# Low halves of eleven weight tiles by a negated copy and an accumulating DMA, and weights asked for two tiles ahead

## The chip, the cores and the metric

One core of a Trainium2 chip runs the whole layer. The metric is the device time of one execution in microseconds (us). The engines in the profile's names: PE (matrix products), DVE (vector operations), ACT (activations and copies), POOL (general purpose; here little more than an issuer of DMAs) and SP (issues most DMAs).

## What is computed

```python
h = rmsnorm(x, g_pre_mix) * (1 + sc1) + sh1            # x: 512 x 1024
proj = h @ w_in                                         # q, k, v of mixers a and b, indexer, two gates
isc = sum_h relu(q_i . k_i) * w_i ; causal ; top_k(isc, 128)
oa = softmax over the selected keys (qa . ka) @ va      # 8 heads of 64, sparse attention "a"
att = exp(log_sigmoid(z) + sum of log_sigmoid(-z) of the later keys)   # z = qb . kb, strictly causal
ob = att @ vb                                           # 8 heads, stick-breaking attention "b"
merged = sigmoid(gate_a) * (oa @ w_up_a) + sigmoid(gate_b) * (ob @ w_up_b)
x = x + ga1 * rmsnorm(merged @ w_out, g_post_mix)
u = relu((rmsnorm(x, g_pre_ffn) * (1 + sc2) + sh2) @ w_ff1)
x = x + ga2 * rmsnorm((u * u) @ w_ff2, g_post_ffn)
```

The six vectors sh1 to ga2 come from silu(c) @ w_ada + b_ada. The top 128 scores of each query row are found as 16 rounds of the eight largest.

## The kernel before

**Products in three parts.** A float32 operand is held as a high half (rounded to the format that PE multiplies) and a low half (what is left). Each product is three matmuls: high by high, high by low, low by high (`mm3`). A weight tile of 128x1024 is loaded by `stage` into one of three buffers `st` (line 109, SP's queue), and `split` makes the halves: ACT copies `st` into `whi` (L113), DVE subtracts, `wlo = st - whi` (L114). There are four buffers each of `whi` and `wlo` (`WBUF`). `wload` does this for one tile; `wnext` hands out the tiles of the list `srcs` in order and loads `AHEAD` = 1 tile further than the one asked for.

**The list of tiles.** First 6 tiles of the v weights (two times three, `V_CUTS`), then by `ORDER = "bbbgbggaggaggg"`: two tiles of w_b for each b (q and k of a pair of b heads), one of w_gate for each g, four of w_a for each a. After those, in the merge, w_gate and w_up for each of 8 column blocks m, and four tiles of w_out.

**The mixer stage** (about 60 to 320 us). Several generators take turns: the main stream of products, the indexer, the units of attention b and of attention a. From 104 us on DVE has two kinds of work. One is the indexer's top 128: per round and for each of three blocks of rows (256, 384 and 512 keys) a MAX8 (L411) and a MATCH_REPLACE8 (L412), and at the end `mask` (L416), which attention a needs. The other is attention b: for each unit (two heads, four blocks b of 128, 256, 384 and 512 keys) ACT writes the two sigmoids `a` (L484) and `be` (L485), DVE scans `a` (L486) and multiplies `be` by it (L488), PE transposes `be` (`tr`, L430), ACT evacuates it to `pT` (L185), and PE multiplies by v. The program code gives the order in which all this is issued, but the layer that records the program sorts each engine's instructions by estimates of its own, so that a change of one instruction can move others.

**The merge stage** (about 320 to 401 us). For each m: PE makes the gate product (24 matmuls into a bank `mm`), then `pb` (12 matmuls with `obh`, `obl`) and `pa` (12 with `oah`, `oal`) from one tile of w_up. Both go into banks of the tag `s`, of which there are three: in this order of use, pb of block m+1 takes the bank of pa of block m-1, and pa of m+1 that of pb of m. DVE reads pb in L676 and pa in L679. Between these DVE has the adaLN columns: up to four tiles of w_ada per m (`LATE`), each loaded through the same three `st` buffers and reduced by one DVE dot product (L213). After the last m come eight transposes (`tr<-identr,ga`), then the product with w_out into four banks; the fourth of these, `s_863`, is the bank that pb of m = 7 had.

The last stages (norm, w_ff1, w_ff2) also use `wload`, and their accumulating DMAs (`wn`, L890; `ub`) are issued by POOL.

Of the kernel before, what the change touches and what calls it, by code (L numbers as in the profile page):

```python
# [7 lines left out]
F32 = mybir.dt.float32  # L8
F32R = mybir.dt.float32r
BF16 = mybir.dt.bfloat16  # L10
AF = mybir.ActivationFunctionType
ALU = mybir.AluOpType
# [3 lines left out]
D = 1024  # L16
# [11 lines left out]
V_CUTS = ((0, 3), (3, 6), (6, 8))  # L28
# [21 lines left out]
EVAC_B = 100  # L50
NORM = 4
ORDER = "bbbgbggaggaggg"
AHEAD = 1
ROWS = 6
IDX_GAP = 1
# [10 lines left out]
def layer_kernel(tc, x, ada, vecs, c_row, rope, w_first, w_v, w_b, w_a, w_gate, w_up, w_out, w_ff1, w_ff2, w_right, out):  # L66
    nc = tc.nc
    es = ExitStack()
    with es:
# [5 lines left out]
        def uid(name):  # L75
            cnt[0] += 1
            return f"{name}_{cnt[0]}"
# [29 lines left out]
        def stage(src, w=D):  # L107
            st = per.tile([P, D], F32, name=uid("st"), tag="st", bufs=3)
            nc.sync.dma_start(st[:, :w], src)
            return st  # L110

        def split(dst_hi, dst_lo, src):
            nc.scalar.activation(dst_hi, src, AF.Copy)  # L113
            nc.vector.tensor_tensor(dst_lo, src, dst_hi.bitcast(F32), op=ALU.subtract)  # L114
# [1 line left out]
        wmore = []  # L116
        turn, wturn = [0], [0]

        def wload(src, w=D):
            st = stage(src, w)  # L120
            wturn[0] = (wturn[0] + bool(wmore)) % (WBUF + 1)
            if wmore and wturn[0] == 0:
                pair = wmore[0].tile([P, 2, D], F32R, name=uid("wx"), tag="ah")
                hi, lo = pair[:, 0], pair[:, 1]
            else:
                hi, lo = [per.tile([P, D], F32R, name=uid(n), tag=n, bufs=WBUF) for n in ("whi", "wlo")]
            split(hi[:, :w], lo[:, :w], st[:, :w])
            return hi, lo

        def scaled_gain(dst, j, g0):  # L130
# [134 lines left out]
        for k in range(KT):  # L265
            if k + 1 < KT:
                prepare(k + 1)
            hi, lo = wfirst[k]
# [223 lines left out]
        srcs = [(w_v[g, i, :, :(k1 - k0) * VREST], (k1 - k0) * VREST) for g in range(2) for i, (k0, k1) in enumerate(V_CUTS)]  # L492
        feeds = {"b": iter(w_b[i] for i in range(8)), "g": iter(w_gate[i] for i in range(8)), "a": iter(w_a[i] for i in range(8))}
        for kind in ORDER:
            srcs += [(next(feeds[kind]), D) for _ in range({"b": 2, "g": 1, "a": 4}[kind])]
# [3 lines left out]
        ready = []  # L499

        def wnext(i=[0]):
            while len(ready) < min(len(srcs), i[0] + 1 + AHEAD):
                ready.append(wload(*srcs[len(ready)]))
            i[0] += 1
            return ready[i[0] - 1]

# [10 lines left out]
        def pair_b(hp):  # L517
            qq = q_pair()
            kk = k_pair()
            def parts(ps, scale):  # L520
                hi, lo = [tp.tile([P, 512], F32R, name=uid(n), tag=n, bufs=2) for n in ("bhi", "blo")]
                nc.scalar.activation(hi, ps, AF.Copy, scale=scale)
                nc.vector.scalar_tensor_tensor(lo, ps, scale, hi.bitcast(F32), op0=ALU.mult, op1=ALU.subtract)
                return [(hi[e * HD:(e + 1) * HD], lo[e * HD:(e + 1) * HD]) for e in range(2)]

            ps = yield from cols_T(wnext())
            for e, (hi, lo) in enumerate(parts(ps, QK_SCALE)):
                r, o = slice(e * HD, (e + 1) * HD), slice((1 - e) * HD, (2 - e) * HD)
                nc.sync.dma_start(qq[r, e].bitcast(F32), hi.bitcast(F32))
                nc.sync.dma_start(qq[o, e].bitcast(F32), lo.bitcast(F32))  # L530
            yield
            ps = yield from cols_T(wnext())
            for e, (hi, lo) in enumerate(parts(ps, 1.0)):
                r, o = slice(e * HD, (e + 1) * HD), slice((1 - e) * HD, (2 - e) * HD)
                nc.sync.dma_start(kk[r, 2 * e].bitcast(F32), hi.bitcast(F32))
                nc.sync.dma_start(kk[o, 2 * e].bitcast(F32), lo.bitcast(F32))
                nc.sync.dma_start(kk[o, 2 * e + 1].bitcast(F32), hi.bitcast(F32))
                nc.sync.dma_start(kk[r, 2 * e + 1].bitcast(F32), lo.bitcast(F32))
            yield

            def ready():
                yield 2
                tens[f"b{hp}"] = [(qq[:, e], kk[:, 2 * e:2 * e + 2]) for e in range(2)]

            spawn(ready())

        def project(dst, scale):
            ws = [wnext(), wnext()]
            for t in range(NT):
                ts = slice(t * P, (t + 1) * P)  # L550
                ps = bank("mm")
                for k in range(KT):
                    hi, lo = ws[k // 4]
                    cs = slice((k % 4) * 256, (k % 4 + 1) * 256)
                    mm3(ps[:, :256], hTh[k][:, ts], hTl[k][:, ts], hi[:, cs], lo[:, cs], k == 0, k == KT - 1)
                    if k == 3:
                        yield
                nc.scalar.activation(dst[:, t], ps[:, :256], AF.Copy, scale=scale)
                if t == NT - 1:
                    do_rope(dst.rearrange("p t (h d) -> p t h d", h=4), 4)  # L560
                yield
# [35 lines left out]
        def main_stream():  # L597
# [4 lines left out]
            nb = ng = na = 0  # L602
            for kind in ORDER:
                if kind == "b":
# [61 lines left out]
        for m in range(KT):  # L666
# [3 lines left out]
            hi, lo = wnext()  # L670
# [50 lines left out]
        for k in range(KT):  # L721
            if k < WOB:
                wo.append(wnext())
            else:
                st = stage(w_out[k])
                hi = wp.tile([P, D], F32R, name=f"woh{k}")
                lo = wp.tile([P, D], F32R, name=f"wol{k}")
# [97 lines left out]
        def token_sums(p):  # L825
            nc.vector.tensor_tensor(blk(p, S3), blk(p, A11), blk(p, S1), op=ALU.subtract)
            nc.vector.tensor_tensor(blk(p, S1), blk(p, S1), blk(p, A22), op=ALU.subtract)
            nc.vector.tensor_tensor(blk(p, S2), blk(p, S1), blk(p, A11), op=ALU.subtract)

        ws = [wload(w_ff1[m]) for m in range(EARLY)]  # L830
        for h in range(2):
            for m in range(EARLY):
# [3 lines left out]
        for m in range(EARLY, MF):  # L836
            ff1(m, wload(w_ff1[m]), 0, NT)
            if m == MF - 1 - WBUF:
                wmore.clear()
            if m % 2:  # L840
                token_sums(m // 2)
                i = (m - 11) // 2
                if 0 <= i < KT:
                    ada_cols(40 + i)
                    gated_gain(KT + i, 40 + i, 72 + i)
                    if i == KT - 1:
                        rows_of(ga2b, ga[:, KT:], evac)
# [138 lines left out]
        for p in range(NP - LAST):  # L986
# [12 lines left out]
            if p in (5, 6):  # L999
                i = p - 5  # L1000
# [135 lines left out]
```

## Time and profile before

| | before |
|---|---|
| median of 3 runs (lowest to highest) | 788.04 us (787.72 to 788.55) |
| the profiled execution: its time, its span | 787.75 us, 785.9 us |
| granted PE clock, mean | 0.998 |
| PE busy, share of the span | 762.7 us, 97% |
| DVE busy | 582.5 us, 74% |
| ACT busy | 406.4 us, 52% |
| POOL busy | 28.6 us, 4% |

The span runs from the first to the last instruction of the profiled execution; its time lies 1.85 us above. Busy matmuls overlap in the profile (each lasts longer than the distance to the next), so the time that PE loses is read from the distances between starts, and from what it waited for.

### The profile page before, as it was taken

To read this page: it belongs to the slowest core of one execution; us is meant where nothing else is said; L and a number is where in the kernel's file an instruction comes from. 1 tells how busy PE (TensorE), PEld (TensorE's weight loads), DVE (VectorE), ACT (ScalarE), POOL (GpSimd) and SP (SyncE) were. 2 spreads that over 40 slices of the span, in tenths; PEclk is the share of its full clock that TensorE was granted. 3 is DMA by queue.
4 is the path that set the end of the run, shared out by engine and by line. 5 is a ranking of instruction groups with operands and counts; after the bars stand their busy time and mean duration, and the time that the engine had idled before them with its cause. 6 is when DMAs were issued, how large, how long until landed. Compare 5 with 4: busy or idle time off the path is not lost.

```text
span 785.9 us, 10955 instructions
## 1 busy us (share of the span) xinstructions
PE 762.7 (97%) x4014; PEld 636.8 (81%) x4014; DVE 582.5 (74%) x1096; ACT 406.4 (52%) x736; POOL 28.6 (4%) x44
## 2 busy tenths in 40 slices
PE   5999999998999999999999999999999999999996
PEld 5889988777889877786778898888888878888885
DVE  6966799999747678678875875554544588888966
ACT  6545546545647578623145863223232368768852
POOL 0000000000000000000000000000000011161000
PEclk9999999999999999999999999999999999999999
DMA  9943266450131210377784254434422189899502
GB/s 349 402 124 90 73 162 174 134 146 30 59 104 54 81 55 28 105 248 251 253 285 170 75 176 152 155 130 144 160 82 81 54 217 218 198 208 262 183 0 108
DMA packets 36437, 117.48 MB, mean 149 GB/s; under 512 B 4640, under 2 KB 4640, under 8 KB 36384
## 3 DMA queue, kind: packets, MB, share of 16 engines
q1 hardware_dynamic: 32064, 105.74, 40.2%
q0 software_dynamic: 4176, 11.01, 8.1%
q8 instruction: 32, 0.52, 0.3%
q14 instruction: 21, 0.17, 0.1%
q10 hardware_dynamic: 144, 0.03, 0.0%
HBM read 108.38 MB, written 2.10 MB: 141 GB/s over the span
## 4 chain that ended last, share of the span: by engine, by line
PE 73%; DVE 16%; DMA 6%; ACT 2%; issue 2%; SPq 0%; DVEq 0%; ACTq 0%
PE mm L140 24%; PE s L140 19%; PE o L140 7%; PE s L870 6%; PE mm L870 5%; PE tr L870 5%; DVE wlo L114 3%; DVE isc L412 3%; DVE sm L411 2%; DVE a L486 2%; DMA st<-in_ada_dram 2%; DMA st<-in_w_up_dram 2%; PE tr L430 2%; DVE st L213 1%; PE tr L140 1%
## 5 line engine op out<-in xcount | busy, mean ns | idle before, releaser
L113 ACT ACTIVATE whi<-st 128x1024 fp32r<-128x1024 f32 (+3 forms) x102 | 102.1, 1003 | 170.1 <-PE mm L140 44.9
L114 DVE TENSOR_TENSOR wlo<-st,whi 128x1024 fp32r<-128x1024 f32 (+3 forms) x102 | 117.3, 1153 | 60.8 <-ACT whi L113 60.7
L140 PE MATMUL mm<-hTh,whi 128*128 128x512 f32 x192 | 77.9, 406 | 0.0
L140 PE MATMUL mm<-hTh,wlo 128*128 128x512 f32 x192 | 75.4, 393 | 0.0
L140 PE MATMUL mm<-hTl,whi 128*128 128x512 f32 x192 | 75.1, 391 | 0.0
L140 PE MATMUL mm<-whi,hTh 128*128 128x256 f32 (+2 forms) x208 | 62.2, 305 | 0.0
L213 DVE CUSTOM_DVE_ANT_0 st<-st,cb,vec 128x1024 f32<-128x1024 f32 x32 | 41.0, 1283 | 26.4 <-DMA st<-in_ada_dram 26.2
L140 PE MATMUL mm<-whi,hTl 128*128 128x256 f32 (+2 forms) x208 | 60.2, 295 | 0.0
L140 PE MATMUL mm<-wlo,hTh 128*128 128x256 f32 (+2 forms) x208 | 60.1, 295 | 0.0
L140 PE MATMUL s<-h2h,whi 128*128 128x512 f32 (+1 forms) x120 | 43.4, 361 | 0.0
L140 PE MATMUL s<-h2l,whi 128*128 128x512 f32 (+1 forms) x120 | 43.3, 361 | 0.0
L140 PE MATMUL s<-h2h,wlo 128*128 128x512 f32 (+1 forms) x120 | 43.3, 361 | 0.0
L140 PEld LDWEIGHTS mm<-hTh,wlo 128*128 128x128 f32 x192 | 36.0, 188 | 7.7
L140 PEld LDWEIGHTS mm<-hTl,whi 128*128 128x128 f32 x192 | 36.2, 188 | 6.3
L140 PEld LDWEIGHTS mm<-hTh,whi 128*128 128x128 f32 x192 | 36.2, 189 | 6.2 <-issue 0.2
L140 PEld LDWEIGHTS mm<-wlo,hTh 128*128 128x128 f32 x208 | 39.5, 190 | 1.1
L140 PEld LDWEIGHTS mm<-whi,hTl 128*128 128x128 f32 x208 | 39.5, 190 | 0.6
L140 PEld LDWEIGHTS mm<-whi,hTh 128*128 128x128 f32 x208 | 39.0, 190 | 0.4
L870 PE MATMUL s<-whi,ah 128*128 128x512 f32 x100 | 36.1, 390 | 0.3 <-ACT whi L113 0.3
L890 POOL DMA_DIRECT2D wn<-in_w_right_dram x13 | 11.4, 874 | 577.6 <-DVE ub L909 528.0
L140 PE MATMUL s<-kT,qT 128*128 128x256 f32 (+2 forms) x128 | 30.6, 345 | 0.9 <-ACT be L485 0.9
L823 DVE TENSOR_TENSOR ub<-ub 128x512 f32<-128x512 f32 (+1 forms) x36 | 22.4, 626 | 10.8 <-ACT ub L822 10.8
(352 smaller groups left out, 1956.2 us busy)
## 6 DMA issues: line engine op xcount, KB each, us to landing
st<-in_w_ff_dram SPq DMA_DIRECT2D x50, 512.0 KB, 3.4
st<-in_ada_dram SPq DMA_DIRECT2D x32, 512.0 KB, 3.8
sa<-in_ada_dram SPq DMA_DIRECT2D x16, 512.0 KB, 8.6
st<-in_w_gate_dram SPq DMA_DIRECT2D x16, 512.0 KB, 3.7
ld<-in_w_ff_dram SPq DMA_DIRECT2D x14, 512.0 KB, 4.5
wn<-in_w_right_dram POOLq DMA_DIRECT2D x13, 512.0 KB, 5.9
st<-in_w_first_dram SPq DMA_DIRECT2D x8, 512.0 KB, 8.9
st<-in_w_b_dram SPq DMA_DIRECT2D x8, 512.0 KB, 3.4
```

The source lines that it names most:

```text
L113: nc.scalar.activation(dst_hi, src, AF.Copy)
L114: nc.vector.tensor_tensor(dst_lo, src, dst_hi.bitcast(F32), op=ALU.subtract)
L140: nc.tensor.matmul(o, lhsT, rhs, start=start, stop=stop)
L213: nc.vector.tensor_tensor_reduce(out=st, in0=st, in1=cb[0], scale=1.0, scalar=vec[:, j:j + 1], op0=ALU.mult, op1=ALU.add, accum_out=mod[:, ...
L411: nc.vector.max(out=m8, in_=cur)
L412: nc.vector.match_replace(out=cur, in_to_replace=m8, in_values=cur, imm_value=SENT)
L430: nc.tensor.transpose(tr[:, j * P:(j + 1) * P], ps[e][:, j * P:(j + 1) * P], ident)
L486: nc.vector.tensor_tensor_scan(a[:, n - 1::-1], a[:, n - 1::-1], zero.to_broadcast([P, n]), 1.0, op0=ALU.mult, op1=ALU.add)
L823: nc.vector.tensor_tensor(u, u, u, op=ALU.mult)
L870: nc.tensor.matmul(acc[i], s[:, ts], m[:, cs], start=f, stop=l, skip_group_check=onto)
L890: nc.gpsimd.dma_start(nw[p], w_right[p], accum_op=ALU.add)
```

## The change

Eleven tiles, number 6 to 16 of the list (the eight of w_b and the first three of w_gate), get their low half in another way: ACT writes `hi = copy(st)` and `lo = copy(-hi)`, and POOL issues a DMA that reads the tile from DRAM once more and adds it onto `lo`. DVE has no part in these tiles. From tile 6 on `wnext` asks two tiles ahead instead of one, in the mixer, in the merge and for w_out.

```diff
+N_V = 2 * len(V_CUTS)
+N_DMA = 11
 AHEAD = 1
...
-        def wload(src, w=D):
+        def wload(src, w=D, low_by_dma=False):
             st = stage(src, w)
...
-            split(hi[:, :w], lo[:, :w], st[:, :w])
+            if low_by_dma:
+                nc.scalar.activation(hi, st, AF.Copy)
+                nc.scalar.activation(lo, hi.bitcast(F32), AF.Copy, scale=-1.0)
+                nc.gpsimd.dma_start(lo, src, accum_op=ALU.add)
+            else:
+                split(hi[:, :w], lo[:, :w], st[:, :w])
             return hi, lo
...
         def wnext(i=[0]):
-            while len(ready) < min(len(srcs), i[0] + 1 + AHEAD):
-                ready.append(wload(*srcs[len(ready)]))
+            while len(ready) < min(len(srcs), i[0] + 1 + (AHEAD if i[0] < N_V else AHEAD + 1)):
+                n = len(ready)
+                ready.append(wload(*srcs[n], N_V <= n < N_V + N_DMA))
             i[0] += 1
             return ready[i[0] - 1]
```

The order of instructions moves at three places that matter here. Line numbers of the changed program are 2 to 8 higher than before (L418 there is L411 here, L419 is L412, L493 is L486, L495 is L488, L684 is L676, L687 is L679), and buffer numbers differ as well.

On DVE in the mixer, the last rows up to the product `be` of the third pair of heads, second head, block of 384 keys; before:

```order
L486 SCALAR_TENSOR_TENSOR a_367_1904<-a_367_1904,zero_87 128x384
L412 MATCH_REPLACE isc_78_585<-sm_425_2191,isc_78_585 128x512
L488 TENSOR_TENSOR be_368_1905<-be_368_1905,a_367_1904 128x383
L411 MAX sm_441_2260<-isc_78_585 128x8
L411 MAX sm_445_2292<-isc_78_585 128x8
L486 SCALAR_TENSOR_TENSOR a_370_1914<-a_370_1914,zero_87 128x384
L412 MATCH_REPLACE isc_78_585<-sm_441_2260,isc_78_585 128x256
L412 MATCH_REPLACE isc_78_585<-sm_445_2292,isc_78_585 128x384
L411 MAX sm_453_2328<-isc_78_585 128x8
L411 MAX sm_457_2365<-isc_78_585 128x8
L412 MATCH_REPLACE isc_78_585<-sm_453_2328,isc_78_585 128x512
L488 TENSOR_TENSOR be_371_1915<-be_371_1915,a_370_1914 128x383
```

and with the change:

```order
L495 TENSOR_TENSOR be_371_1922<-be_371_1922,a_370_1921 128x383
L418 MAX sm_480_2502<-isc_78_585 128x8
L493 SCALAR_TENSOR_TENSOR a_373_1931<-a_373_1931,zero_87 128x384
L419 MATCH_REPLACE isc_78_585<-sm_480_2502,isc_78_585 128x512
L418 MAX sm_491_2560<-isc_78_585 128x8
L418 MAX sm_492_2569<-isc_78_585 128x8
L419 MATCH_REPLACE isc_78_585<-sm_491_2560,isc_78_585 128x256
L419 MATCH_REPLACE isc_78_585<-sm_492_2569,isc_78_585 128x384
L418 MAX sm_496_2596<-isc_78_585 128x8
L495 TENSOR_TENSOR be_374_1932<-be_374_1932,a_373_1931 128x383
L419 MATCH_REPLACE isc_78_585<-sm_496_2596,isc_78_585 128x512
L423 TENSOR_SCALAR mask_606<-isc_78_585 128x256
```

The same `be` (`be_371` before, `be_374` now) stands behind 14, 13 and 13 MAX8 (256, 384, 512 keys) and 13, 13 and 13 MATCH_REPLACE8 before, and behind 16, 16 and 16 and 16, 16 and 15 now; of the splits since the first MAX8 there are 9 before and 3 now.

On SP in the merge, the loads through the three `st` buffers for one m; before:

```order
L109 DMA st_783_3898<-in_w_up_dram 128x1024
L109 DMA st_787_3930<-in_w_gate_dram 128x1024
L109 DMA st_792_3968<-in_ada_dram 128x1024
L109 DMA st_793_3972<-in_ada_dram 128x1024
L109 DMA st_794_3976<-in_ada_dram 128x1024
L109 DMA st_795_3980<-in_ada_dram 128x1024
```

and with the change:

```order
L111 DMA st_773_3829<-in_w_gate_dram 128x1024
L111 DMA st_777_3861<-in_w_up_dram 128x1024
L111 DMA st_782_3899<-in_ada_dram 128x1024
L111 DMA st_783_3903<-in_ada_dram 128x1024
L111 DMA st_784_3907<-in_ada_dram 128x1024
L111 DMA st_785_3911<-in_ada_dram 128x1024
```

In each round of six the w_up tile is now that of the next m, so that it comes a whole round earlier for PE; one w_up tile more stands ahead of the first w_ada tiles.

On DVE at the end of the merge, around the read of the last pb (L676, now L684); before:

```order
L114 TENSOR_TENSOR wlo_841_4270<-st_839_4267,whi_840_4269 128x1024
L213 ISA st_844_4305,mod_91<-st_844_4305,cb_746_3652,vec_65 128x1024
L213 ISA mod_91 128x1
L114 TENSOR_TENSOR wlo_849_4341<-st_847_4338,whi_848_4340 128x1024
L676 TENSOR_TENSOR mrg_748_3657<-s_843_4274,mrg_748_3657 128x512
```

and with the change:

```order
L116 TENSOR_TENSOR wlo_844_4287<-st_842_4284,whi_843_4286 128x1024
L220 ISA st_847_4322,mod_91<-st_847_4322,cb_749_3669,vec_65 128x1024
L220 ISA mod_91 128x1
L116 TENSOR_TENSOR wlo_852_4358<-st_850_4355,whi_851_4357 128x1024
L684 TENSOR_TENSOR mrg_751_3674<-s_846_4291,mrg_751_3674 128x512
```

The read of the last pb keeps its place behind the same number of loads; only the tiles are others (w_out 1 and 2 instead of 0 and 1).

## Rows read from the trace of the kernel before

**Rows 1.** What PE waited for: us in total, times, longest.

```profile
PE tr L430 <- ACT pT L185: 3.5, 3, 2.8
...
PE s L140 <- DVE wlo L114: 2.1, 4, 0.5
PE s L140 <- ACT whi L113: 1.3, 3, 0.7
```

**Rows 2.** Busy time per engine in two stretches: PE, PEld, DVE, ACT, POOL, clock, DMA.

```profile
104.00:200.00 96.00, 91.81 (x527) 73.43 (x527) 95.75 (x223) 49.68 (x117) 0.60 (x2) 1.00 0.45 124
335.00:401.00 66.00, 62.44 (x266) 48.96 (x265) 53.30 (x86) 16.78 (x23) 0.00 (x0) 1.00 0.78 254
```

**Rows 3.** Timeline of PE at the longest wait in the mixer: start, duration, [idle before].

```profile
184.26 0.88 PE L430 MATMUL tr<-identr,be 128*128 128x128 f32 x6 [2.76 <-ACT pT L185]
```

**Rows 4.** Timeline of ACT ahead of that wait.

```profile
180.93 0.60 ACT L485 ACTIVATE be<-s 128x512 f32<-128x512 f32 x1 [2.35 <-DVE be L488]
```

**Rows 5.** Chain of waits, 100 to 200 us: start, length, link.

```profile
104.20 0.79 DVE sm L411 x2
104.99 0.92 DVE isc L412 x2
105.91 0.92 DVE sm L411 x2
106.83 1.06 DVE isc L412 x2
...
111.45 1.05 DVE sm L411 x2
...
164.50 1.12 DVE wlo L114
...
193.91 1.19 DVE isc L412 x2
```

**Rows 6.** Timeline of DVE as the indexer's top 128 begins.

```profile
100.76 1.23 DVE L114 TENSOR_TENSOR wlo<-st,whi 128x1024 fp32r<-128x1024 f32 x1 [0.86 <-ACT whi L113]
...
104.13 0.87 DVE L411 MAX8 sm<-isc 128x8 f32<-128x256 f32 x2
```

**Rows 7.** Timeline of ACT: high half of tile 10, an evacuation, high half of tile 13.

```profile
99.67 1.06 ACT L113 ACTIVATE whi<-st 128x1024 fp32r<-128x1024 f32 x1 [0.55 <-PE mm L140]
100.63 0.58 ACT L522 ACTIVATE bhi<-mm 128x512 fp32r<-128x512 f32 x1
...
117.85 1.06 ACT L113 ACTIVATE whi<-st 128x1024 fp32r<-128x1024 f32 x1 [1.00 <-PE mm L140]
```

**Rows 8.** The accumulating DMAs of `wn`, 512 KB each: ns on POOL, and landing.

```profile
L890 POOL DMA_DIRECT2D wn<-in_w_right_dram x13: 862/862/1011, 632.6 to 692.7; - x13
...
DMA to landing us min/median/max: 5.4/5.9/7.9
```

**Rows 9.** Loads into `st` from 326 to 396 us: landing, min/median/max.

```profile
DMA to landing us min/median/max: 3.2/4.3/5.3
```

**Rows 10.** Timeline of PE in the merge and into the w_out product.

```profile
340.63 0.39 PE L140 MATMUL mm<-hTh,whi 128*128 128x512 f32 x1
...
346.07 0.39 PE L140 MATMUL s<-obh,whi 128*128 128x512 f32 x1
...
401.01 1.03 PE L154 MATMUL tr<-identr,ga 128*128 128x128 f32 x8
...
403.95 0.39 PE L140 MATMUL s<-whi,mgh 128*128 128x512 f32 x1
```

**Rows 11.** Timeline of DVE at the start and the end of the merge.

```profile
324.30 1.23 DVE L162 TENSOR_TENSOR cb<-cb,cs 128x1024 f32<-128x1024 f32 x1 [0.80 <-ACT cs L161]
...
402.95 0.68 DVE L676 TENSOR_TENSOR mrg<-s,mrg 128x512 f32<-128x512 f32 x1
```

**Rows 12.** Timelines of SP and PE: last copy of the first `kT`, and its first use.

```profile
112.46 0.59 SPq L538 DMA_DIRECT2D kT<-blo  x1
...
116.01 0.28 PE L140 MATMUL s<-kT,qT 128*128 128x256 f32 x1
```

## The prediction

> **What bounds the kernel now.** I read the first part of the page (PE is busy nearly all the span), then the list of PE's waits, then busy time by stretch, then the chain of waits and the timelines at the places that these name. The list shows where PE can still gain: it waited for ACT's evacuation of the transposed `be` of attention b (3.5 us, one wait of 2.8), and in the merge for the halves of a w_up tile (2.1 and 1.3 us) [rows 1]. The change touches both. The stretches show that the limits there differ [rows 2]. From 104 to 200 us DVE is busy 95.75 of 96 us, so PE's waits there come from DVE's queue: the longest ends at 184.26 [rows 3], and ahead of it ACT's next sigmoid had waited 2.35 us for DVE's `be` of 383 keys, which ended at 180.9 [rows 4]. From 335 to 401 DVE is busy 53 of 66 us, and the loads through three `st` buffers set the pace.
>
> The list understates the merge. 24 matmuls of a gate product take 346.07 - 340.63 = 5.44 us, 0.2267 each; from the first matmul of pb of m = 3 to the transposes are 216 matmuls, 48.96 us, but 54.94 pass [rows 10]. So 5.98 us are lost there, the slow restart after each wait included. That is the largest sum that the second half of the change could win.
>
> **The mixer, part by part.** Gone from DVE are eleven splits; six of them lay between the first MAX8 (104.13) and the `be` that ends at 180.9, nine before and three now (orders above). In the chain one split counts 1.12 us [rows 5], so 6.7 us leave this queue. But the order also shows what takes their place. Ahead of the same `be` there are now 2 more MAX8 of 256 keys, 3 more of 384, 3 more of 512, and 3, 3 and 2 more MATCH_REPLACE8. The chain has them in pairs [rows 5]: MAX8 0.79 (256 with 384), 0.92 (512 with 256), 1.05 (384 with 512); MATCH_REPLACE8 0.92, 1.06 and 1.19 in the same pairs. That is 0.79 + 0.92 + 2 x 1.05 = 3.81 and 2 x 0.92 + 1.06 + 1.19 = 4.09, together 7.9. So the queue ahead of this `be` grows by 7.9 - 6.7 = 1.2 us: the freed time goes to the top 128, whose mask comes earlier, and nothing waits for the mask there. Against this, the top 128 can begin earlier. The split at 100.76 goes [rows 6], and the instruction behind it needs only ACT's evacuation, which ends at 100.63 + 0.58 = 101.2 [rows 7] instead of 101.9: 0.6 us. Net the `be` ends 0.6 us later, and ACT's order between it and PE's transposes is the same, so the wait of 2.76 us ends 0.6 later. Waits before it are absorbed in it. Later ones shrink, since from the next pair of heads on the top 128 is finished and all 6.7 us are gained; of the two small waits in the 3.5 [rows 1], 0.7 together, I count 0.3 as gone. Mixer: +0.3 us. Bounds: -4 if the relief did reach PE, +3 if ACT's inserted copies leave DVE waiting three times for a copy of 1.06.
>
> **What is added.** Eleven negating copies on ACT, each like a `whi` (1.06 us [rows 7]); ACT is busy 50 of 96 us in the stretch [rows 2], and no copy stands between the late `be` and PE's wait. Cost nothing. The DMAs: the nearest rows are those of `wn`, the same 512 KB added onto a tile: 0.86 us on POOL, 5.9 to landing, 7.9 at most [rows 8]. Cover: the high half of tile 10 is written at 99.67, as soon as PE has released tile 6's buffers; the product of tile 10 follows that of tile 9, which ends just before tile 13's half is written at 117.85 [rows 7]. Of these 18.2 us the two copies take 2.1, the place of the second copy in ACT's order at most one product (6.1, a third of the 18.2), POOL 0.9, landing 5.9: 15.0. About 3 us are left at worst, 9 when the second copy follows at once. Cost nothing, on this cover. POOL's own other work there is three selections on the indexer's scores, between which one DMA stands; 0.9 us at most, and I take nothing, since the selection behind it serves only the third MAX8.
>
> **The merge.** The w_up halves now come a round of six loads earlier, so the five waits of [rows 1] on `wlo` and their companions on `whi` vanish, and PE could reach the transposes 5.98 us sooner. The ring itself doesn't run faster: six loads through three buffers are two landings (4.3 us median [rows 9]) with one split and one dot product behind them, and none of that waits for PE. And the product with w_out, after the transposes, needs a fourth bank, `s_863`, which pb of m = 7 had; its release is DVE's read L676, which stands in DVE's order behind the same ring loads as before. Before, that read ended at 402.95 + 0.68 = 403.63 [rows 11], and PE's first matmul into the bank came at 403.95 [rows 10], 0.3 later, without a wait. So PE, almost 6 us early, stops there until the read is done. The ring starts later now: one more w_up tile's split is ahead of DVE's multiplication at 324.30, 1.12 us, of which 0.80 fill idle time [rows 11]: +0.3. The read ends at 403.9, PE goes on at 404.0. Six us of waits vanish and one wait of about the same length takes their place: merge +0.1 us. Bounds: each load's landing can be a us off its median [rows 9], which passes to PE in full; -1.5 to +1.
>
> Behind this, w_out's own tiles come a slot earlier, and the later stages run as before.
>
> Sum: +0.3 + 0.1 = +0.4 on the profiled 787.75; the median of the three runs lies 0.29 above it, so 788.4 us. About 0.2% (1.6 us) is what a measurement can tell from no change; this is within it.
>
> **The rivals.**
>
> 1. The relief works. DVE has no slack in this stretch, and the order is by the recorder's estimates; if the chip's `be` came earlier nonetheless, because MAX8 rows are skipped over by waits of their own, the 3.5 us and most of a further us behind them go: 788.04 - 4.4 + 0.1 = about 783.7. Against it: an engine runs its order, and the counts are plain. The Trainium skill, "Perfetto Trace Analysis", Optimizing Scalar/DVE Operations, says that work may be moved to Scalar when DVE is saturated; by that alone the 6.7 us would be PE's as far as it waits. The trace agrees that DVE is saturated (95.75 of 96 us); what the freed time is spent on the rule doesn't say. 0.09.
>
> 2. The merge keeps part of its 6 us, because the ring, whose splits of w_up and gate stand in another order, ends 1.5 to 3 us sooner; then 785.4 to 786.9. For it: landings of 3.2 occur [rows 9]. Against: order and dependences of the ring are otherwise the same. 0.13.
>
> 3. Slower: the copies of `kT`. The last of the first set is issued at 112.46 and used at 116.01 [rows 12], 3.55 us later, and tile 11's accumulating DMA is under way just then. It decides if the copy then takes over 3.55 us; if it landed like `wn` after 5.9, PE would stop for 2.4 us and attention b, which feeds the saturated DVE, would begin that much later: 790.8. 0.13.
>
> 4. Slower: the accumulating DMAs land late. It decides above 5.9 + 3 = 9 us; each tile is triggered by the release of the tile four before, so that 2 us too many cost 2 us twice or three times over: 792 to 795. Against it: 7.9 is the maximum of 13 [rows 8]. The Trainium skill, "SBUF — State Buffer", on two separate sides ("DVE blocks DMA" trap), says that GpSimd can't write the descriptors of its DMAs while DVE holds the port that they share in certain modes. The rows of `wn` show 862 to 1011 ns on POOL, no sign of it; they come from a stretch where DVE was less busy than here. 0.07.
>
> **How the numbers follow.** The forecast has 0.58, with a range of its own of 787.2 to 789.9 (ring -1 to +1, mixer -0.5 to +1); most of it is within 1.6 us of 788.04, 0.05 of it above. Rivals 1 to 4 have 0.09, 0.13, 0.13, 0.07. Faster: 0.09 + 0.11 of rival 2 = 0.20. Slower: 0.13 + 0.07 + 0.05, less 0.02 of rival 3 that stays within = 0.23. Same: 0.57. The range reaches to rival 2's low end, 785.4, and to rival 3's 790.8; outside are rival 1, rival 4 and the edges of 2 and 3, a little under 0.2.
>
> **What would show it.** Right: the list of PE's waits loses `wlo` L114 and `whi` L113 of the merge and gains one of about 6 us (5 to 6.5) on DVE's read of pb (now L684) near 398 to 404; the transposes of the merge begin near 395.5; the mask is written 11 us earlier than 195; the wait of 2.8 on `pT` is still there, ending near 184.9. Wrong: a `be` of the third pair that ends before 180; a transpose wait under 2 us; no wait at the w_out bank; a `wlo` of tiles 6 to 16, or a `kT`, in PE's list.

## The result, and the profile after

The changed kernel takes 797.58 us (median of 4 runs, 797.25 to 799.08), beside 787.88 (787.65 to 788.55) for the kernel before on the same chip: ratio 1.0127, 95% interval 1.0115 to 1.0139. It is 9.7 us slower; I had forecast 788.4 and a range to 790.8. The profiled execution has a span of 795.4 us, 9.5 more than before.

What PE waited for, in the changed kernel; it answers to [rows 1]:

```profile
PE tr L437 <- ACT pT L192: 4.5, 2, 3.9
...
PE s L147 <- DMA kT<-bhi: 3.8, 1, 3.8
PE s L147 <- DVE mrg L684: 3.8, 1, 3.8
...
PE mm L147 <- ACT mrg L677: 0.7, 1, 0.7
...
PE s L147 <- DMA kT<-blo: 0.6, 1, 0.6
```

The merge's `wlo` and `whi` are gone, as the change means it. The copies of `kT`, on which PE never stopped before, are in the list, and the wait for `pT` has grown. The places, in PE's timeline of the changed kernel; the rows answer to [rows 3, 10, 12]:

```profile
113.25 0.39 PE L147 MATMUL mm<-hTh,wlo 128*128 128x512 f32 x1
117.41 0.55 PE L147 MATMUL s<-kT,qT 128*128 128x256 f32 x1 [3.77 <-DMA kT<-bhi]
118.52 0.55 PE L147 MATMUL s<-kT,qT 128*128 128x256 f32 x1 [0.56 <-DMA kT<-blo]
...
191.19 0.69 PE L437 MATMUL tr<-identr,be 128*128 128x128 f32 x2 [3.86 <-ACT pT L192]
...
353.95 0.39 PE L147 MATMUL s<-obh,whi 128*128 128x512 f32 x1
...
402.91 1.04 PE L161 MATMUL tr<-identr,ga 128*128 128x128 f32 x8
...
405.36 0.50 PE L147 MATMUL mm<-whi,mgh 128*128 128x512 f32 x1 [0.72 <-ACT mrg L677]
...
410.76 0.79 PE L147 MATMUL s<-whi,mgh 128*128 128x512 f32 x1 [3.75 <-DVE mrg L684]
```

In the kernel before, the last product ahead of the first `kT`, and that first use (PE's timeline):

```profile
114.15 0.39 PE L140 MATMUL mm<-hTh,wlo 128*128 128x512 f32 x1
114.38 0.40 PE L140 MATMUL s<-kT,qT 128*128 128x256 f32 x2
```

Ahead of the wait that ends at 191.19, `be` on DVE and two of ACT's sigmoids behind it, from the timelines of these two engines ([rows 4] has the first of these sigmoids before):

```profile
186.36 0.54 DVE L495 TENSOR_TENSOR be<-be,a 128x383 f32<-128x383 f32 x1
...
186.93 0.60 ACT L492 ACTIVATE be<-s 128x512 f32<-128x512 f32 x1 [2.73 <-DVE be L495]
...
189.78 0.60 ACT L492 ACTIVATE be<-s 128x512 f32<-128x512 f32 x1 [0.82 <-DVE be L495]
```

The second of them in the kernel before, where it had no wait:

```profile
182.85 0.60 ACT L485 ACTIVATE be<-s 128x512 f32<-128x512 f32 x1
```

Busy time by stretch in the changed kernel (columns as in [rows 2]); the first two rows answer to it:

```profile
104.00:200.00 96.00, 86.50 (x460) 68.74 (x459) 84.11 (x205) 50.63 (x113) 5.19 (x6) 0.95 0.65 164
335.00:401.00 66.00, 66.00 (x293) 54.66 (x292) 54.56 (x92) 17.63 (x24) 0.00 (x0) 1.00 0.76 250
100.00:115.00 15.00, 13.64 (x61) 10.93 (x59) 14.66 (x41) 8.67 (x12) 4.18 (x6) 1.00 1.05 281
...
116.00:118.00 2.00, 0.55 (x1) 0.29 (x1) 0.49 (x2) 0.00 (x0) 0.00 (x0) 0.50 1.08 212
118.00:120.00 2.00, 1.48 (x5) 1.23 (x6) 0.45 (x3) 0.45 (x2) 0.00 (x0) 0.50 1.01 255
...
191.00:193.00 2.00, 1.81 (x9) 1.81 (x10) 1.90 (x3) 1.42 (x5) 0.00 (x0) 0.50 0.40 127
...
410.00:412.00 2.00, 1.24 (x3) 1.05 (x4) 1.97 (x5) 1.06 (x1) 0.00 (x0) 0.50 0.82 279
```

And the stretch from 100 to 115 us in the kernel before, same view:

```profile
100.00:115.00 15.00, 15.00 (x70) 12.50 (x70) 14.24 (x35) 6.84 (x11) 1.55 (x3) 1.00 0.60 151
```

Two columns are new to the story. The DMA share of this stretch went from 0.60 to 1.05. The share adds up the times of the packets; since rows above 1 occur, 1 isn't its hard top, but by this measure the sixteen DMA engines are crowded. And the granted clock falls to 0.50 (1.2 of 2.4 GHz) behind each of the three long waits of PE.

To see where the time went I set the start of the same PE instruction in the two traces side by side (the difference is called the lag).

- **Before the first `kT`.** The lag is -0.9 from 20 us on (113.25 against 114.15 in the rows): the changed kernel's trace runs ahead there, long before its first accumulating DMA. The traces of the experiments stand at -0.7 to +1.0 at this place, so I take it for a difference between executions.
- **The copies of `kT`.** The two waits (4.33) and the matmuls at half clock behind them (2.7) bring the lag to 6.1.
- **The late transposes.** At those of 184.26 it is 191.19 - 184.26 = 6.93, 0.9 more than just ahead of them. The `be` of 383 keys isn't the cause: it ends at 186.90, 6.0 later than before, no more than PE was late itself. The 0.9 came behind it, where ACT's second sigmoid waited 0.82 for DVE's next `be`. Half clock adds 1.45, and 0.5 comes back near 208 us: 7.9 when the mixer is done.
- **The merge** gives 5.98 back (353.95 - 346.07 = 7.88, then 402.91 - 401.01 = 1.90).
- **In front of w_out** the two waits for evacuations bring it to 410.76 - 403.95 = 6.81, and half clock 2.7 more: 9.53, which stays to the end.

So 6.8 us are matmuls at half clock, in three places, against a net loss of 9.5.

### The profile page after: what moved, and what is told of

It reads as the page before. It is cut to its first block, busy times and chain, and to the rows that moved or that the text cites. A ratio compares the mean times of both kernels' runs of the same rounds, so it can differ in the third digit from the quotient of the medians.

```text
span 795.4 us, 10990 instructions
## 1 busy us (share of the span) xinstructions
PE 766.4 (96%) x4014; PEld 641.5 (81%) x4014; DVE 571.3 (72%) x1085; ACT 416.1 (52%) x747; POOL 38.2 (5%) x55
## 4 chain that ended last, share of the span: by engine, by line
PE 78%; DVE 10%; DMA 7%; ACT 3%; issue 2%; SPq 0%; DVEq 0%; ACTq 0%
PE mm L147 29%; PE s L147 19%; PE o L147 7%; PE s L878 6%; PE mm L878 5%; PE tr L878 5%; DMA st<-in_ada_dram 2%; PE tr L437 2%; DVE wlo L116 2%; DVE isc L419 1%; DVE sm L418 1%; DVE st L220 1%; PE tr L147 1%; PE tr L343 1%; DMA st<-in_w_up_dram 1%
## 5 line engine op out<-in xcount | busy, mean ns | idle before, releaser
L115 ACT ACTIVATE whi<-st 128x1024 fp32r<-128x1024 f32 (+3 forms) x91 | 90.4, 996 | 156.1 <-DMA st<-in_w_gate_dram 35.8
L116 DVE TENSOR_TENSOR wlo<-st,whi 128x1024 fp32r<-128x1024 f32 (+3 forms) x91 | 103.9, 1145 | 61.9 <-ACT whi L115 61.9
L493 DVE TENSOR_TENSOR_SCAN a<-a,zero 128x128 f32<-128x128 f32 (+3 forms) x32 | 25.6, 811 | 13.0 <-ACT a L491 13.0
```

What stands on the lines that cost most here:

```text
L493: nc.vector.tensor_tensor_scan(a[:, n - 1::-1], a[:, n - 1::-1], zero.to_broadcast([P, n]), 1.0, op0=ALU.mult, op1=ALU.add)
```

## The experiments

The kernel before was timed with each group: 787.98 us (e1, e2, e3, e5), 787.78 (e6, e8, e9, e10), 787.96 (e11, e12, e14, e16). Ratios are against it. The first group ran on another chip than the two others.

### The two halves apart

**e1** asks for weights early but leaves all splits on DVE; **e2** has the DMAs and asks one tile ahead everywhere.

```diff
 e1:
-N_DMA = 11
+N_DMA = 0
 e2:
-            while len(ready) < min(len(srcs), i[0] + 1 + (AHEAD if i[0] < N_V else AHEAD + 1)):
+            while len(ready) < min(len(srcs), i[0] + 1 + AHEAD):
```

> No low half by DMA (N_DMA = 0), two tiles ahead kept. Theory T (the accumulating DMAs' traffic delays the copies of kT): no wait on kT, the mixer as before, and at 335 us PE stands within 0.5 us of before; in the merge the five small waits on the w_up halves are gone, and one wait of 3.5 to 4 us for DVE's read of pb comes at the fourth w_out bank, with the granted clock at 0.5 for some 5 us after it; about +1.5, so 789 to 790. Rival O (the loads asked for earlier on SP's queue make kT late): the wait on kT stays, 794 to 796.

> Low halves of eleven tiles by DMA, one tile ahead as before. T: the wait on kT of about 4 us with the clock drop behind it, mixer +7 to +9 at 335 us; the merge as before with its small waits; 795 to 797. Rival O: no wait on kT, 788 to 789.

e1: 788.31 us, 1.0002 (0.9991 to 1.0012). e2: 795.22, 1.0094 (1.0074 to 1.0114). In e2 PE waits 2.9 us for `kT` and its lag is 7.6 at 208.9, 7.0 from 396. So 7.2 of the 9.7 us come with the DMAs alone and 0.3 with the earlier asking alone; about 2 appear only with both (e14). In e1 the merge gives 5.98 us, and the two waits ahead of w_out take 4.4 back; most of the rest goes to the clock (e10).

### What of the DMAs costs the time

**e3** leaves the second read out: the low half is the negated high half.

```diff
-                nc.gpsimd.dma_start(lo, src, accum_op=ALU.add)
```

> The changed kernel without the accumulating DMAs: the low half of the eleven tiles is left at the negated high half, all else (ACT's copies, DVE's order, two ahead) as changed. T: no wait on kT, its copies land in 2.2 to 2.5 us again; the wait on pT in the third pair of heads ends 0.6 to 0.9 later than before and may cost a clock drop; with the merge's +1.5 in all 789.5 to 791.5. Rival A (the reordering of DVE and ACT's extra copies cause most of the loss): 795 to 798.

789.34 us, 1.0022 (1.0007 to 1.0036). No wait for `kT`; DMA share 0.60 from 100 to 115, copies of `kT` landing in 2.2 to 3.8 us. ACT's eleven extra copies and DVE's new order cost about 1 us together (789.34 - 788.31, e1; the two spreads overlap). In e3's trace the mixer has none of it: the lag is 1.0 at 125 us and 1.0 at 335, and the wait at the w_out bank is 4.8 us, where e1 has 4.0. The read costs the rest, 8.2 us.

**e6** keeps the read, on the same queue and of the same size, but without adding (the low half then holds the weights).

```diff
-                nc.gpsimd.dma_start(lo, src, accum_op=ALU.add)
+                nc.gpsimd.dma_start(lo, src)
```

> The changed kernel with the second read of the eleven tiles left on the same queue and of the same size, but writing over the low half in place of adding to it (the low half then holds the weights themselves; only that is wrong in the output). Two theories of what made everything on the DMA rings land in 7 to 9 us. A, the accumulation: without it the copies of kT land in 2 to 3.5 us as in the kernel before, the kT wait of 3.8 us is gone, and the time is that of the kernel with the low half left negated and no second read, 789.3 (788 to 791). B, the bytes and the queue alone (5.8 MB more through GpSimd's queue): the copies of kT land in 7 to 9 us as in the changed kernel, and the time is 796 to 798.

796.21 us, 1.0107 (1.0090 to 1.0124): theory A, that the adding is the cause, fell. How long the copies of `kT` took to land (min, median, max, issues from 105 to 123 us), in the kernel before:

```profile
DMA to landing us min/median/max: 2.2/2.3/2.5
```

In the changed kernel:

```profile
DMA to landing us min/median/max: 7.3/8.8/9.3
```

In e6:

```profile
DMA to landing us min/median/max: 4.2/6.8/7.1
```

The adding makes the landing about 2 us longer, but a plain read is enough: PE waits 2.6 us for `kT` in e6. What a transfer takes of the engines stands in the page's list of queues (packets, MB, share of sixteen engines' span). The kernel before:

```profile
q1 hardware_dynamic: 32064, 105.74, 40.2%
q0 software_dynamic: 4176, 11.01, 8.1%
```

The changed kernel, whose eleven DMAs are the difference in q0:

```profile
q0 software_dynamic: 5760, 16.78, 11.9%
```

(0.119 x 795.4 - 0.081 x 785.9) / 11 = 2.8 us of all sixteen engines for one accumulating DMA; 1.9 for e6's plain one (10.7%); 1.6 for 512 KB on SP's queue (q1). Three of them are issued from 100 to 115 us: 3 x 2.8 / 15 = 0.56, on top of the 0.60 that was there. That is 1.16 by this sum; 1.05 was measured.

**e12** tests this by size: each DMA over half of the columns (the other half of the low part stays the negated high half). **e16** tests the place: only tiles 10 to 12, those three. **e8** does the opposite, tiles 6 to 9.

```diff
 e12:
-                nc.gpsimd.dma_start(lo, src, accum_op=ALU.add)
+                nc.gpsimd.dma_start(lo[:, :w // 2], src[:, :w // 2], accum_op=ALU.add)
 e16:
-                ready.append(wload(*srcs[n], N_V <= n < N_V + N_DMA))
+                ready.append(wload(*srcs[n], N_V + 4 <= n < N_V + 7))
 e8:
-N_DMA = 11
+N_DMA = 4
```

> The changed kernel, each of the eleven accumulating DMAs over half of the columns only (256 KB in place of 512; the other half of the low part stays the negated high half). Theory, the transfers' volume: with three accumulating DMAs of 512 KB in the stretch from 100 to 115 us the sixteen DMA engines have more to move than they can (share 1.05, against 0.60 before); with half of it the share falls to 0.8 to 0.9, the first copies of kT land in 3 to 5.5 us in place of 7 to 9, PE's wait for kT is 0 to 1.5 us, and the time is 789 to 792. Rival: any accumulating DMA under way delays everything, whatever its size: landings of 6 us and more, kT wait above 2.5 us, 794.5 to 797.

> The changed kernel with accumulating DMAs for the tiles 10, 11 and 12 only (three in place of eleven). Theory: the loss belongs to the place, the first copies of kT, and these three transfers are the ones under way there; so three of eleven bring nearly all of it: kT waits of 3 to 4.4 us, DMA share above 0.9 from 100 to 115, 793.5 to 797. Rival: each DMA costs its part: 788.3 + 3/11 of 9 = 790.7 or less.

> The changed kernel with four accumulating DMAs (w_b tiles 6 to 9) in place of eleven, all issued before the first kT copies. If the loss comes from accumulating DMAs that are under way just when the first kT copies are issued (my theory), there is no kT wait above 0.5 us and the time is that of the kernel with the earlier asking alone, 788.3, up to 1 us more for the other order of DVE: 787.5 to 790. If the loss goes with their number (a rate, each DMA costing its part), four elevenths of 7.2 to 9 us: 790.6 to 791.5.

e12: 789.72 us, 1.0026 (1.0007 to 1.0044). Its ten times go from 787.59 to 791.92, five of them above 790.9 at a mean clock of 0.991; the trace is of one at 788.09 (0.993). It has one wait for `kT`, of 0.4. Its stretch, DMA share 0.92, above the 0.8 to 0.9 that I expected (0.60 + 3 x 1.6 / 15 by its own q0 row would be 0.92):

```profile
100.00:115.00 15.00, 14.63 (x67) 11.89 (x66) 14.40 (x40) 9.08 (x14) 4.18 (x6) 1.00 0.92 230
```

and the landing of its `kT` copies:

```profile
DMA to landing us min/median/max: 2.2/3.5/5.2
```

e16: 795.52 us, 1.0102 (1.0085 to 1.0119). Three DMAs of eleven bring 7.6 us, most of the loss; its DMA share from 100 to 115 is 0.86, though, below the 0.9 that I expected. Its list of waits:

```profile
PE s L147 <- DVE mrg L684: 4.1, 1, 4.1
PE s L147 <- DMA kT<-blo: 4.1, 2, 2.2
...
PE tr L437 <- ACT pT L192: 2.4, 1, 2.4
```

e8: 789.11 us, 1.0015 (1.0001 to 1.0029), no wait for `kT`. Its own four reads slow other transfers too (the `qT` copies land in 5 to 6 us), but they are over when the copies of `kT` are issued:

```profile
DMA to landing us min/median/max: 2.2/2.3/3.4
```

So most of the loss belongs to three transfers at one place, not to a rate for each.

The share from 100 to 115 us doesn't put these runs in order: e8, without a wait, has more than e16. Over the microseconds in which the first copies of `kT` are issued and awaited, 106 to 118 (a window chosen afterwards), it does so much better:

| run | DMA share, 100 to 115 us | 106 to 118 us | PE's wait for `kT`, us |
|---|---|---|---|
| before | 0.60 | 0.65 | none |
| e1 | 0.59 | 0.64 | none |
| e3 | 0.60 | 0.65 | none |
| e8 | 0.94 | 0.81 | none |
| e12 | 0.92 | 0.87 | 0.4 |
| e6 | 0.91 | 0.97 | 2.6 |
| e16 | 0.86 | 1.00 | 4.1 |
| e2 | 1.05 | 1.07 | 2.9 |
| changed | 1.05 | 1.07 | 4.3 |
| e14 | 1.06 | 1.07 | 4.4 |

That the copies' packets stand behind those of the reads in the sixteen engines is the likely way; no view here shows it.

### The mixer: why DVE's relief gives nothing

**e11** is e3 with 13 of the 16 rounds of the top 128, so that DVE's order has no more rounds ahead of the late `be` than before, and six splits fewer.

```diff
-            for i in range(TOPK // 8):
+            for i in range(TOPK // 8 - 3):
```

> The kernel with eleven negated low halves and no second read, and with 13 of the 16 rounds of the top 128 (the top 104, so the mask is another one). Now as many rounds stand ahead of the be of 383 keys in DVE's order as in the kernel before (13), and six splits fewer. Theory (step of the prediction: the freed time goes to the top 128, and only therefore nothing comes of it at PE): this be ends 6 to 7 us earlier than in the kernel with 16 rounds, PE's wait of 2.8 to 3.0 us for pT near 184 falls under 0.5, and the time is 3 to 4.4 us below that kernel's 789.3: 785 to 786.3. Rival: PE's wait has another cause (ACT's own order, PE's banks), it stays above 2 us, 788.5 to 789.5.

785.59 us, 0.9975 (0.9963 to 0.9987), 3.75 below e3. The later `be` of the pair in e3's timeline of DVE:

```profile
181.85 0.54 DVE L494 TENSOR_TENSOR be<-be,a 128x383 f32<-128x383 f32 x1
```

and in e11's:

```profile
174.86 0.56 DVE L494 TENSOR_TENSOR be<-be,a 128x383 f32<-128x383 f32 x1 [0.35 <-ACT be L491]
```

7.0 us earlier, of which 1.3 is a difference of the two executions that stands from 20 us on. The wait near 184 (2.95 in e3) is gone, one of 1.3 for `pT`, earlier, is left in its list, and PE reaches the transposes of 184.26 at 181.27, 3.0 before the kernel before. So the relief is worth 3 to 4 us here, and the top 128 takes it.

### The merge: a bank, a split and the clock

**e10** is e1 with sixteen matmuls that nobody reads, in front of the matmul that waits for its bank. It asks whether the clock falls there because PE stands still.

```diff
+FILL_MM = 16
...
+                    if (k, t, n) == (0, 1, 1):
+                        fill = bank("o")
+                        for _ in range(FILL_MM):
+                            mm(fill, hTh[0][:, :P], hTh[1], True, True)
```

> Weights asked for two tiles ahead without any accumulating DMA, and sixteen matmuls of 128x512 added (3.6 us of work that nobody reads, into a bank of its own) just before the w_out matmul that waits 4.0 us for its bank. Theory: the granted clock fell to 0.5 behind that wait since PE stood still for 3.8 to 4 us, and this cost 2.6 us; with PE busy there the clock stays at 1.0 behind it and the time is 785.2 to 786.5 (2.6 below the same kernel without the added matmuls, 788.3). Rival: the clock falls there for another reason (then the row of the windows still shows 0.5 near 412, and the time is 788 to 789.5).

789.02 us, 1.0015 (1.0003 to 1.0027): not the time that I expected, but the clock did what the theory says. e1's stretches:

```profile
400.00:402.00 2.00, 0.00 (x0) 0.00 (x0) 1.26 (x2) 0.71 (x1) 0.00 (x0) 0.80 0.85 268
402.00:404.00 2.00, 1.38 (x3) 1.17 (x4) 1.97 (x4) 1.13 (x2) 0.00 (x0) 0.50 0.97 365
404.00:406.00 2.00, 2.00 (x6) 1.56 (x5) 1.90 (x3) 0.84 (x2) 0.00 (x0) 0.50 0.96 303
```

e10's, with PE busy:

```profile
400.00:402.00 2.00, 1.70 (x8) 1.12 (x7) 2.00 (x3) 1.06 (x1) 0.00 (x0) 1.00 0.58 193
402.00:404.00 2.00, 2.00 (x11) 1.60 (x10) 1.97 (x4) 0.63 (x1) 0.00 (x0) 1.00 0.71 246
404.00:406.00 2.00, 2.00 (x10) 1.68 (x9) 1.90 (x4) 1.35 (x2) 0.00 (x0) 1.00 0.47 135
```

This trace is of an execution at 787.22; the twelve times go from 786.74 to 791.24, most of them at a mean clock a little below its 0.999, so it doesn't show what the longer ones met. In it PE keeps 2.39 us of lead behind the bank (start 401.56, before 403.95); at 455 us it has 0.45 left. The next wait takes it, 1.7 us on DVE's `h2f` at the second norm. In the median the sixteen matmuls gain nothing.

**e5** takes the bank away instead: the fourth w_out bank comes from tag "o". **e9** does that too and gives out the third weight buffer of the feed-forward stage only behind the w_out stage.

```diff
 e5 and e9, on e1:
-        yt = [[bank(a), bank(b)] for a, b in (("mm", "mm"), ("s", "s"))]
+        yt = [[bank(a), bank(b)] for a, b in (("mm", "mm"), ("s", "o"))]
...
-        w_out_tile(2, ("s", "o"))
+        w_out_tile(2, ("s", "s"))
 e9 only:
-        wmore.append(x1p)
...
+        wmore.append(x1p)
```

> e1 with the fourth w_out bank taken from the tag o instead of s (and the next row block's second bank from s), so that it needs no read of pb. Theory M (the merge's gain was given back at this bank): the wait for DVE's read is gone, PE keeps most of the 6 us, less 1 to 2 us of waits for the third w_out tile, no clock drop: 783 to 785. Rival: the ring of loads sets the end of the w_out product anyway, and the wait moves to its tiles in full: 787 to 789.

> Weights asked for two tiles ahead without any accumulating DMA, the fourth w_out bank taken from another tag, and the third weight buffer of the feed-forward stage given out only behind the w_out stage, so that DVE's queue doesn't stand behind that load's split ahead of the first yg. If that split was what held DVE in the run before it (theory: PE keeps the merge's gain once nothing in DVE's order waits for a load there), PE keeps 3.5 to 5 us and the time is 783 to 785.5, and no wait on h2f of more than 1.5 us. Rival: the next thing in the order (first transposes of the second norm, which need all of w_out's tile on ACT and DVE) or a later feed-forward load takes it back: 787 to 789.

e5: 789.31 us, 1.0017 (1.0003 to 1.0030), not the 783 to 785 that I expected. The wait at the bank is gone, and a wait of 4.1 on `h2f` stands some 35 us later, ending at 438.2, with the clock at 0.50 behind it. The cause is in DVE's timeline:

```profile
423.07 1.23 DVE L116 TENSOR_TENSOR wx<-st,wx 128x1024 fp32r<-128x1024 f32 x1 [5.97 <-ACT wx L115]
424.21 0.68 DVE L709 TENSOR_TENSOR yg<-mm,ga1b 128x512 f32<-128x512 f32 x1
```

DVE stands 6 us in front of the split of a feed-forward weight that isn't loaded yet (ACT's copy of it waits 6.14 us for the load), and the evacuation of w_out's first tile (`yg`) is queued behind it: at 424.21, later than the 422.55 of the kernel before, though PE was 3.6 to 5 us early. In e9 the split stands further back, and the first `yg` is at 418.53:

```profile
418.53 0.69 DVE L709 TENSOR_TENSOR yg<-mm,ga1b 128x512 f32<-128x512 f32 x1 [2.17 <-ACT jk L708]
```

e9: 783.57 us, 0.9951 (0.9937 to 0.9966), 4.2 us faster than the kernel before; a wait of 1.0 on `mrg` and one of 0.7 on `xn` are all that the merge and the second norm still cost PE, and the clock stays at 1.00. It keeps the earlier asking and drops the accumulating DMAs.

**e14** puts e9's two edits on the changed kernel with all eleven DMAs.

> The changed kernel, all eleven accumulating DMAs, with the two changes of the merge that let PE keep its gain (fourth w_out bank of another tag, third weight buffer of the feed-forward stage given out behind the w_out stage). If the two halves of the change add up, it is the 783.6 of the kernel with these and without the DMAs, plus what the DMAs alone cost (795.2 - 788.0 = 7.2): 790 to 791.5. If the merge's gain hangs on the mixer's end (later loads, fewer under way), 787 to 789 or 792 to 794.

793.26 us, 1.0070 (1.0053 to 1.0086), above what I expected, though not for the rival's reason: the edits of the merge give 4.3 here (797.58 - 793.26) and 4.7 without DMAs (788.31 - 783.57), so they add up whenever the mixer ends. What doesn't is my price of the DMAs: 7.2 when tiles are asked for one ahead (e2), but 9.3 and 9.7 two ahead (797.58 - 788.31, 793.26 - 783.57). The traces put most of this at `kT`: the lag grows there by 5.5 us in e2, with the clock at 0.50 for 3.4, and by 7.0 in the changed kernel and 7.6 in e14, with 0.50 for 6.8. Why the clock stayed low longer isn't shown.

## Why the prediction failed, step by step

- **"What is added", failed.** "Cost nothing, on this cover." The cover that I worked out was that of the low half itself, and it held: the five accumulating DMAs issued from 96 to 128 us landed in 6.8 to 9.9 us, median 9.1, and no low half of tiles 6 to 16 is in PE's list. What I didn't count is what the transfers take from others. From 100 to 115 us they crowd the sixteen engines (1.05), the copies of `kT` land in 7.3 to 9.3 us in place of 2.2 to 2.5, and 3.55 us of cover [rows 12] is gone. PE lost 7.0 us there, 4.33 waiting and 2.7 at half clock. e3, e6, e12 and e16 show it: with no read, the read plain, half of it, three of them. A `kT` in PE's list was also the prediction's own sign of being wrong.
- **Rival 3 named the place but not the size.** I let a copy land like one `wn` DMA, 5.9 [rows 8], for 2.4 us of wait. PE waited 4.33, and at the first half of the set already (copies issued from 106.86 to 109.41), not only at the last copy; rival 3 had no clock in it either. The whole came to 7.2 (e2). The numbers for a better price were on the page before: q0 gives 0.081 x 785.9 us for 11.01 MB, 3.0 us of all engines for 512 KB, three times in a stretch whose share was 0.60.
- **Rival 4 didn't decide.** Landing beyond 9 us did occur, but no tile was late for its own product by it.
- **POOL's issue and the shared port, right.** These DMAs took 862 to 877 ns on POOL while DVE was busy 14.66 of 15 us. The Trainium skill's "DVE blocks DMA" trap ("SBUF — State Buffer", SBUF: two separate sides), which I weighed there, doesn't show; whether DVE's instructions here hold the shared port isn't in the trace.

From the tile's view of the changed kernel, for these two points:

```profile
L132 POOL DMA_DIRECT2D wlo<-in_w_b_dram x4: 862/869/877, 96.8 to 127.8; - x4
...
DMA to landing us min/median/max: 6.8/9.1/9.9
```

- **The mixer's own term: right in e3, near by luck in the changed kernel.** Forecast +0.6 at the late transposes and -0.3 behind. e3 has this order without the reads, and there these transposes come 0.5 later (a lag of 1.5, of which 1.0 was there from 20 us on), with 0.5 back behind them. In the changed kernel the +0.9 comes from ACT's second sigmoid, between the late `be` and PE's transposes, where the prediction had ACT's order unchanged. e11 shows the cause in DVE's order, and so that rival 1's relief is real but spent.
- **The merge, right in mechanism, two sizes off.** (The prediction reads five waits on `wlo` out of [rows 1]; the rows have four, and three on `whi`.) 216 matmuls from 353.95 to 402.91 are 48.96 us, just the working time that I had counted, so all of the 5.98 was won. The wait at the w_out bank came, but as 4.0 in e1, since DVE's read of pb started at 401.88, 1.07 earlier than before, where I had it 0.3 later:

```profile
400.74 1.23 DVE L116 TENSOR_TENSOR wlo<-st,whi 128x1024 fp32r<-128x1024 f32 x1 [1.88 <-ACT whi L115]
401.88 0.68 DVE L684 TENSOR_TENSOR mrg<-s,mrg 128x512 f32<-128x512 f32 x1
```

  Rival 2 had a ring that ends earlier for its gain. The clock took it away: in e1 PE is 1.33 us early at the bank and 1.36 late a few microseconds on. The term of +0.1 was nearly right for e1 (+0.3) by two errors that cancel.
- **The clock, missing.** The prediction prices each wait by its length. The one long wait that I had looked at, 2.76 [rows 3], leaves the clock at 1.00, and I took it as the pattern for all. In the changed kernel 6.8 us are lost to matmuls at half clock, against 9.5 in all. The Trainium skill, "TensorE: Matmul & The Clock Gate", "HAM oscillation — how this bites in real kernels", says that a PE which waits for DMA between bursts is throttled to half rate and starts the next burst cold. The rows of the three long waits agree, for waits on DMA, on ACT and on DVE alike; e10, with PE kept busy, is at 1.00. Some shorter waits here didn't lower it (last section).

## What to carry to other kernels

A transfer that nobody waits for isn't free: price it in engine time (its bytes by its queue's share in the page) and look at every small copy that will be under way beside it and has only a few us of cover. Add the price to the DMA share of just the microseconds in which such copies are under way: here 0.81 cost nothing, 0.87 a wait of 0.4 us, 0.97 and more 2.6 to 4.4. Three reads at such a place cost most of what eleven did. Where a wait is taken away, ask what stands next in the order of the engine that PE will then wait for (here a bank, then a split of a feed-forward weight), and follow it until nothing in that order waits for a load. And a wait that ended in a clock at 0.50 cost its length and 1.4 to 2.7 us more in the changed kernel.

## What I had not expected of the hardware

- Reads of 512 KB on GpSimd's queue, one every 5 to 6 us, delayed SP's copies of 128 KB by 4 to 5 us even when they added nothing (e6). The Trainium skill, "DMA: Bandwidth & Descriptors", "Issuing engines are not separate DMA queues", says that transfers of all issuers run on the same sixteen engines and interleave; the landings agree, and put a size on it: 2.3, 6.8 and 8.8 us (medians) with none, plain and accumulating reads beside them. Whether the same bytes on SP's own queue would do as much was not tried; with a single load of 512 KB on it directly ahead of the copies (e3) they landed in 2.2 to 3.8 us.
- One accumulating DMA of 512 KB took 2.8 us of all sixteen engines, a plain one on the same queue 1.9, 512 KB on SP's queue 1.6 (by the page's shares).
- Waits of nearly one length leave the clock in different states. The one for `pT` was 2.76 (before), 2.77 (e1) and 2.95 (e3) with the clock at 1.00 behind it, and 2.43 (e16) and 2.93 (e12) with 0.50 behind it. In e6 two waits for `kT` of 1.2 and 1.0, close together, left 0.50 as well. The waits of 3.5 us and more in the mixer, the merge and behind it left 0.50, all of them. What decides it for the shorter ones these runs don't settle.
